# Prompt attention scores: two heads in the two row halves of the array, three products of 64 rows, no stacked copies

## The chip, the cores and the metric

The kernel runs on one core of one Trainium2 chip. The metric is device time in microseconds of one execution. The kernel before took 1777.86 us, the median of three runs (1774.98 to 1778.14).

## The reference

One inference step of a two-layer decoder trunk in float32: a prompt of 512 tokens and 8 sampled sequences of 8 new tokens each, which the kernel joins to T = 64 + 512 token columns. Each layer mixes tokens by three groups of heads (dilated attention with 8 heads of 64, two gated linear attentions), then applies a convolutional feed-forward part. The change touches the prompt's attention scores alone, the first product here:

```
s = jnp.einsum('nrbqhd,nrbkhd->nrbhqk', qb, kk) * (Dh ** -0.5)
...
s = jnp.where(valid[:, None], s + bias, -jnp.inf)
lse = jax.nn.logsumexp(s, axis=-1)
o = jnp.einsum('nrbhqk,nrbkhd->nrbqhd', jnp.exp(s - lse[..., None]), vv)
```

The three dilated branches are merged by their softmax denominators; the kernel gets the same from one softmax over all causal keys, with a bias that holds the slopes and the logarithm of how many branches read a key.

## The kernel before, in words

Features lie on the 128 partitions, tokens along the columns. A projection is a sum over 8 feature tiles. For near-float32 accuracy both operands are split into a high part in `F32R` and a low part, the difference, and three products are summed (`gemm`, lines 126 to 128): high x high, high x low, low x high. Weights come by DMA into `wraw`, ScalarE makes the high part (L107) and VectorE the low part (L108).

`mixing` first makes the gated linear heads (`hgrn_head`, `gla_tile`), then loops over four pairs of attention heads (`for p in range(4)`). A pair's 128 features are two heads of 64, the first on partitions 0 to 63, the second on 64 to 127. Per pair:

- the queries `qp` (128 x 512, evacuated at L796 and L798) and the keys `ka` (128 x 576, L574) are projected;
- the split copies for the score products are made. Before the change the two parts of a query are stacked on the partitions: for head `hb`, `q2[:, hb]` holds the high part on the head's own 64 partitions (ScalarE, L815) and the low part on the other 64 (GpSimd, L818). `kh[:, hb]` holds the high part of the keys on both halves (ScalarE, L816 and L817), `kl[:, hb]` the low part on both (GpSimd, L819 and L820). All three have one buffer, so the copies for a pair wait for the last score product of the pair before it;
- for each block `i` of 128 query rows and each head, two products on all 128 rows of the array (L832) give the scores of n = 128 (i + 1) keys: one with `kh` sums high x high and low x high, one with `kl` sums high x low and low x low;
- softmax of a block: VectorE adds the bias and takes the maximum (L839), negates it (L841), ScalarE takes the exponential with its sum (L842), VectorE the reciprocal (L843) and the multiplication by it (L844);
- TensorE transposes the block (L848), ScalarE and VectorE copy the transposes (L853, L851), and TensorE multiplies by the values (L857) into the head's half of the columns;
- then the sampled tokens' attention over the cached keys and values (L877, L881, L886 to L926), whose products use 32 columns of the array each.

The order on each engine is made ahead of time by a scheduler, which simulates the kernel: it takes the instructions as they become ready, so work of one pair, of the next pair's projections and of the cached keys is interleaved. Engines then run their lists in order. The score products and the levels of the gated linear heads share two PSUM banks of the kind `s`.

Of the kernel before, what the change touches and what calls it, by code (L numbers as in the profile page):

```python
# [8 lines left out]
F32 = mybir.dt.float32  # L9
F32R = mybir.dt.float32r  # L10
I32 = mybir.dt.int32
U8 = mybir.dt.uint8
AF = mybir.ActivationFunctionType
ALU = mybir.AluOpType
# [5 lines left out]
P = 128  # L20
# [3 lines left out]
TS = 64  # L24
TP = 512
# [48 lines left out]
def trunk_kernel(ctx: ExitStack, tc: tile.TileContext, I, O):  # L74
    nc = tc.nc
    V, S, G, PE, SP = nc.vector, nc.scalar, nc.gpsimd, nc.tensor, nc.sync
# [8 lines left out]
    def bank(tag, bufs):  # L85
        return ps.tile([P, 512], F32, name=f"ps_{tag}", tag=tag, bufs=bufs)
# [4 lines left out]
    def s_bank():  # L91
        return bank("s", 2)

    def t_bank():
        return bank("t", 2)

    def o_bank():
        return bank("o", 1)
# [46 lines left out]
    def mark(name, mm):  # L145

        placed[name] = mm.ins
# [415 lines left out]
    def mixing(l, act, first):  # L563
# [16 lines left out]
        with ExitStack() as mx:  # L580
            mp = mx.enter_context(tc.tile_pool(name=f"mp{l}", bufs=1, reuse_waits="tile"))
            ap = mx.enter_context(tc.tile_pool(name=f"ap{l}", bufs=1, reuse_waits="tile"))
# [197 lines left out]
            for p in range(4):  # L780
                qp = ap.tile([P, TP], F32, name="qp", tag="qp", bufs=QKB)
# [19 lines left out]
                ka = ap.tile([P, T], F32, name="ka", tag="ka", bufs=2)  # L801
# [4 lines left out]

                q2 = ap.tile([P, 2, TP], F32R, name="q2", tag="q2", bufs=1)  # L810
                kh = ap.tile([P, 2, TP], F32R, name="kh", tag="kh", bufs=1)
                kl = ap.tile([P, 2, TP], F32R, name="kl", tag="kl", bufs=1)
                for hb in range(2):
                    r, o_ = (slice(64 * e, 64 * e + 64) for e in (hb, 1 - hb))
                    S.activation(q2[r, hb, :], qp[r, :], AF.Copy)  # L815
                    S.activation(kh[r, hb, :], ka[r, TS:], AF.Copy)  # L816
                    S.activation(kh[o_, hb, :], ka[r, TS:], AF.Copy)  # L817
                    G.tensor_tensor(q2[o_, hb, :], qp[r, :], q2[r, hb, :].bitcast(F32), ALU.subtract)  # L818
                    G.tensor_tensor(kl[r, hb, :], ka[r, TS:], kh[r, hb, :].bitcast(F32), ALU.subtract)  # L819
                    G.tensor_tensor(kl[o_, hb, :], ka[r, TS:], kh[r, hb, :].bitcast(F32), ALU.subtract)  # L820
                o = o_bank()
                wb = []
                for hb in range(2):
# [1 line left out]
                    mark(f"d{p}.b{hb}", SP.dma_start(wb[hb], I["pbias"][2 * p + hb]))  # L825
                for i in range(4):
                    n = (i + 1) * P
                    sb, pi, pT = [], [], []
                    for hb in range(2):
                        sb.append(s_bank())  # L830
                        for j, kk in enumerate((kh, kl)):
                            mm = PE.matmul(sb[hb][:, :n], q2[:, hb, i * P:(i + 1) * P], kk[:, hb, :n],  # L832
                                           start=j == 0, stop=j == 1)
                    mark(f"p{p}.{i}", mm)
                    for hb in range(2):
                        pi.append(sp.tile([P, 512], F32, name="pi", tag="pi", bufs=4))
                        w = pi[hb][:, :n]
                        mx_ = sp.tile([P, 4], F32, name="mx", tag="mx", bufs=8)
                        V.tensor_tensor_reduce(w, sb[hb][:, :n], wb[hb][:, 512 - n:512], 1.0, -3.0e38,  # L839
                                               ALU.add, ALU.max, mx_[:, 0:1])  # L840
                        V.tensor_scalar(mx_[:, 1:2], mx_[:, 0:1], -1.0, None, ALU.mult)  # L841
                        S.activation(w, w, AF.Exp, bias=mx_[:, 1:2], accum_out=mx_[:, 2:3])  # L842
                        V.reciprocal(mx_[:, 3:4], mx_[:, 2:3])  # L843
                        V.tensor_scalar(w, w, mx_[:, 3:4], None, ALU.mult)  # L844
                    for hb in range(2):
                        tb = t_bank()
                        for c in range(i + 1):
                            PE.transpose(tb[:, c * P:(c + 1) * P], pi[hb][:, c * P:(c + 1) * P], ident)  # L848
                        pT.append(sp.tile([P, 512], F32, name="pT", tag="pT", bufs=3))
                        if hb:  # L850
                            V.tensor_copy(pT[hb][:, :n], tb[:, :n])  # L851
                        else:
                            S.activation(pT[hb][:, :n], tb[:, :n], AF.Copy)  # L853
                    for c in range(i + 1):
                        for hb in range(2):
                            h = 2 * p + hb
                            PE.matmul(o[64 * hb:64 * hb + 64, i * P:(i + 1) * P], va[:, c, h * 64:(h + 1) * 64],  # L857
                                      pT[hb][:, c * P:(c + 1) * P], start=c == 0, stop=c == i)
# [12 lines left out]
                for half in range(2):  # L871
                    sb = s_bank()
                    sb2.append(sb)
                    for s in range(2):
                        kc = cache(I["ck"][l, p, half, s], f"k{half}{s}")
                        for i in range(4):
                            PE.matmul(sb[32 * i:32 * i + 32, :384], qs[:, 2 * i + s, :], kc[:, i, :],  # L877
                                      start=(s == 0), stop=(s == 1))
                for s in range(2):
                    for i in range(4):  # L880
                        mm = PE.matmul(sb[32 * i:32 * i + 32, 384:448], qs[:, 2 * i + s, :], ka[:, 0:TS],  # L881
                                       start=(s == 0), stop=(s == 1))
# [17 lines left out]
                mm = PE.transpose(tb[:TS, 256:384], pr[:, 768:832], ident)  # L900
# [4 lines left out]
                for s in range(2):  # L905
# [7 lines left out]
                    for i in range(4):  # L913
                        mm = PE.matmul(ob[32 * i:32 * i + 32, s * P:(s + 1) * P],
                                  sT[:TS, 768 + 32 * i:768 + 32 * i + 32], vas[:TS, p * P:(p + 1) * P],
                                  start=False, stop=True)
# [21 lines left out]
        for c in range(KT):  # L938
            col_tile(load_w(I["w_o"][l, c], 5 * P, name=f"wo{c}"), mh, ml, range(5),
                     lambda b, hf, t0, n, c=c: S.activation(y[c][:, t0:t0 + n], b[:, :n], AF.Copy))  # L940

        xpool = right_pool(f"x_{l + 1}")
        src = I["x"] if l == 0 else xdr
# [136 lines left out]
    for l in range(L):  # L1080
        xpool.release()
        ypool.release()
        y, ypool, xpool, act, first = mixing(l, act, first)
        act, first = ffn(l, y, act, first)
# [192 lines left out]
```

## Time and profile before

| What | Value |
|---|---|
| median of the three runs | 1777.86 us |
| profiled execution, its own time | 1782.31 us |
| its span | 1780.5 us |
| TensorE, products | 1703.4 us busy, 96% |
| VectorE | 1136.0 us, 64% |
| ScalarE | 745.9 us, 42% |
| GpSimd | 414.9 us, 23% |
| mean granted clock of TensorE | 0.978 |

Busy times are unions of an engine's instructions. A product's bar runs until its result is out, so the bars of neighbours overlap; how much TensorE spends on one product is read from the distance of two starts. A product of float32 operands appears as two passes in the trace, one of `F32R` operands as one. The form of a product names the part of the array first: 64*32 means 64 rows and 32 columns.

### The profile page before, as it was taken

The numbers are of one execution on the slowest core, as the hardware profiler recorded it, in microseconds if no ns is written. First come the engines' busy times: TensorE is split into PE (matmuls) and PEld (weight loads), VectorE is DVE, ScalarE is ACT, GpSimd is POOL, SyncE is SP. The second block draws the span as 40 slices with busy tenths as digits, with TensorE's granted clock in tenths as the row PEclk, the third lists the DMA queues.
The fourth block names the chain that finished last, engine by engine and source line by source line (L and its number), as shares of the span: only waits on it lengthen the run. The fifth ranks groups of instructions, "written<-read, shape, count | busy, mean of one in ns | idle before, by whom it ended". The sixth has DMA issues, their size and how long they took to land.

```text
span 1780.5 us, 36320 instructions
## 1 busy us (share of the span) xinstructions
PE 1703.4 (96%) x14688; PEld 1598.8 (90%) x14688; DVE 1136.0 (64%) x2515; ACT 745.9 (42%) x1265; POOL 414.9 (23%) x748
## 2 busy tenths in 40 slices
PE   7999989999899999999989999999998999999996
PEld 7888976689799999999988898867898999999996
DVE  6776665655885376476677757466568744754666
ACT  5654424554443333233456534154545433332331
POOL 3544321301420010010254534122024100100103
PEclk9999999999999999999989999899999999999998
DMA  5212225866262562542322222368553526527321
GB/s 176 73 60 69 86 76 210 310 221 246 98 213 79 191 225 83 213 178 73 108 86 86 65 64 88 116 222 307 203 211 130 187 75 236 187 75 270 124 90 54
DMA packets 64520, 260.95 MB, mean 147 GB/s; under 512 B 9536, under 2 KB 15968, under 8 KB 62816
## 3 DMA queue, kind: packets, MB, share of 16 engines
q1 hardware_dynamic: 64352, 258.62, 41.5%
q8 instruction: 116, 1.90, 0.4%
q14 instruction: 52, 0.43, 0.1%
HBM read 245.39 MB, written 80.31 MB: 183 GB/s over the span
## 4 chain that ended last, share of the span: by engine, by line
PE 83%; DVE 10%; ACT 4%; issue 2%; DMA 1%; POOL 0%; SPq 0%; POOLq 0%; DVEq 0%; ACTq 0%
PE ps_m L126 23%; PE ps_m L128 23%; PE ps_m L127 23%; PE ps_s L472 2%; DVE xl L297 2%; PE ps_o L857 1%; PE ps_s L832 1%; PE ps_o L911 1%; DVE y L338 1%; DVE work L417 1%; PE ps_m L622 1%; PE ps_t L848 1%; DMA wraw<-in_w_s 1%; DVE wlo L108 1%; PE ps_s L877 1%
## 5 line engine op out<-in xcount | busy, mean ns | idle before, releaser
L126 PE MATMUL ps_m<-xh,whi 128*128 128x256 f32 (+1 forms) x2240 | 673.9, 301 | 3.1 <-DVE work L574 2.0
L127 PE MATMUL ps_m<-xl,whi 128*128 128x256 f32 (+1 forms) x2240 | 671.8, 300 | 0.0
L128 PE MATMUL ps_m<-xh,wlo 128*128 128x256 f32 (+1 forms) x2240 | 669.8, 300 | 1.2 <-DVE wlo L108 1.2
L126 PEld LDWEIGHTS ps_m<-xh,whi 128*128 128x128 f32 x2240 | 430.8, 192 | 11.4 <-issue 6.1
L127 PEld LDWEIGHTS ps_m<-xl,whi 128*128 128x128 f32 x2240 | 431.2, 192 | 3.0 <-issue 1.9
L128 PEld LDWEIGHTS ps_m<-xh,wlo 128*128 128x128 f32 x2240 | 430.2, 192 | 4.0 <-issue 1.5
L107 ACT ACTIVATE whi<-wraw 128x1024 fp32r<-128x1024 f32 (+3 forms) x224 | 221.4, 991 | 384.8 <-PE ps_m L127 323.5
L108 DVE TENSOR_TENSOR wlo<-wraw,whi 128x1024 fp32r<-128x1024 f32 (+3 forms) x224 | 257.6, 1152 | 183.6 <-ACT whi L107 183.1
L126 PE MATMUL ps_m<-hh,whi 128*128 128x320 f32 (+1 forms) x704 | 208.7, 296 | 1.3 <-DVE y L370 1.3
L128 PE MATMUL ps_m<-hh,wlo 128*128 128x320 f32 (+1 forms) x704 | 208.0, 296 | 0.0
L127 PE MATMUL ps_m<-hl,whi 128*128 128x320 f32 (+1 forms) x704 | 207.6, 295 | 0.0
L126 PEld LDWEIGHTS ps_m<-hh,whi 128*128 128x128 f32 x704 | 132.5, 188 | 1.6 <-DVE y L370 1.6
L127 PEld LDWEIGHTS ps_m<-hl,whi 128*128 128x128 f32 x704 | 133.2, 189 | 0.0
L128 PEld LDWEIGHTS ps_m<-hh,wlo 128*128 128x128 f32 x704 | 132.2, 188 | 0.0
L993 DVE TENSOR_TENSOR u<-ps_m,rbc 128x256 f32<-128x256 f32 x84 | 35.5, 424 | 111.3 <-PE ps_m L128 111.2
L408 POOL TENSOR_TENSOR lev<-work 128x288 f32<-128x288 f32 (+1 forms) x60 | 50.0, 834 | 155.9 <-DVE work L720 39.6
L1029 ACT ACTIVATE hh<-c 128x64 fp32r<-128x64 f32 x88 | 34.2, 436 | 122.3 <-DVE c L1019 122.3
L1001 POOL COPY cso<-u 128x2 f32<-128x2 f32 x88 | 34.5, 392 | 205.8 <-DVE u L993 204.9
L983 POOL COPY u<-cso 128x16 f32<-128x16 f32 x88 | 24.0, 275 | 221.2 <-DVE u L989 178.2
L1009 DVE SCALAR_TENSOR_TENSOR c<-u,par,c 128x592 f32<-128x592 f32 x88 | 73.4, 834 | 2.6
L126 PE MATMUL ps_m<-whi,xh 128*128 128x256 f32 (+1 forms) x256 | 74.2, 290 | 0.0
L127 PE MATMUL ps_m<-wlo,xh 128*128 128x256 f32 (+1 forms) x256 | 73.4, 287 | 0.0
(286 smaller groups left out, 2866.1 us busy)
## 6 DMA issues: line engine op xcount, KB each, us to landing
wraw<-in_w_up SPq DMA_DIRECT2D x88, 512.0 KB, 3.6
kv<-in_ck SPq DMA_DIRECT2D x32, 768.0 KB, 6.9
kv<-in_cv SPq DMA_DIRECT2D x32, 768.0 KB, 6.5
out_ck<-in_ck SPq DMA_DIRECT2D x32, 768.0 KB, 7.0
out_cv<-in_cv SPq DMA_DIRECT2D x32, 768.0 KB, 6.4
wraw<-in_w_s SPq DMA_DIRECT2D x42, 512.0 KB, 3.4
wraw<-in_w_dn SPq DMA_DIRECT2D x32, 448.0 KB, 3.3
wraw<-in_w_v SPq DMA_DIRECT2D x12, 512.0 KB, 3.4
```

Of the source, the lines that this page charges most:

```text
L107: S.activation(hi[:, :n], raw[:, :n], AF.Copy)
L108: V.tensor_tensor(lo[:, :n], raw[:, :n], hi[:, :n].bitcast(F32), ALU.subtract)
L126: PE.matmul(out, ah, bh, start=(i == 0), stop=False)
L127: PE.matmul(out, ah, bl, start=False, stop=False)
L128: PE.matmul(out, al, bh, start=False, stop=(i == n - 1))
L297: V.scalar_tensor_tensor(self.l[k][:, t0:t0 + n], xt[k][:, t0:t0 + n], gnorm(l, which, k), self.h[k][:, t0:t0 + n].bitcast(F32), ALU.mult, ...
L408: G.tensor_tensor(ev[:, :, 0, :], ref, bv[:, :, 0, :], ALU.subtract)
L472: mm = PE.matmul(bp[64 * hh:64 * hh + 64, cp * nh * 32:(cp + 1) * nh * 32], xk[:, c0:c0 + 64], moving(c0), start=True, stop=True)
L993: V.tensor_tensor(u[:, 338:594], b[:, :n], R[:, t0:t0 + n], ALU.mult)
L1001: G.tensor_copy(cso[:, ui, 16:18], u[:, NU - 2:NU])
L1009: V.scalar_tensor_tensor(c, u[:, 2:NU], wc(2), c, ALU.mult, ALU.add)
L1029: S.activation(dh, src, AF.Copy)
```

## The change

`q2`, `kh` and `kl` with a plane for each head are replaced by four tiles `qh`, `ql`, `kh`, `kl` of 128 x 512, with both heads on their own partitions. ScalarE makes each high part in one instruction on 128 partitions, GpSimd each low part. A score block is now the sum of three products (high x high, high x low, low x high) on the 64 rows of the array on which the head lies; the low x low product is gone. In the text the heads alternate inside each of the three products.

```
-                q2 = ap.tile([P, 2, TP], F32R, name="q2", tag="q2", bufs=1)
-                kh = ap.tile([P, 2, TP], F32R, name="kh", tag="kh", bufs=1)
-                kl = ap.tile([P, 2, TP], F32R, name="kl", tag="kl", bufs=1)
-                for hb in range(2):
-                    r, o_ = (slice(64 * e, 64 * e + 64) for e in (hb, 1 - hb))
-                    S.activation(q2[r, hb, :], qp[r, :], AF.Copy)
-                    S.activation(kh[r, hb, :], ka[r, TS:], AF.Copy)
-                    S.activation(kh[o_, hb, :], ka[r, TS:], AF.Copy)
-                    G.tensor_tensor(q2[o_, hb, :], qp[r, :], q2[r, hb, :].bitcast(F32), ALU.subtract)
-                    G.tensor_tensor(kl[r, hb, :], ka[r, TS:], kh[r, hb, :].bitcast(F32), ALU.subtract)
-                    G.tensor_tensor(kl[o_, hb, :], ka[r, TS:], kh[r, hb, :].bitcast(F32), ALU.subtract)
+                qh, ql, kh, kl = (ap.tile([P, TP], F32R, name=m, tag=m, bufs=1) for m in ("qh", "ql", "kh", "kl"))
+                for hi, lo, src in ((qh, ql, qp), (kh, kl, ka[:, TS:])):
+                    S.activation(hi, src, AF.Copy)
+                    G.tensor_tensor(lo, src, hi.bitcast(F32), ALU.subtract)
...
-                    sb, pi, pT = [], [], []
-                    for hb in range(2):
-                        sb.append(s_bank())
-                        for j, kk in enumerate((kh, kl)):
-                            mm = PE.matmul(sb[hb][:, :n], q2[:, hb, i * P:(i + 1) * P], kk[:, hb, :n],
-                                           start=j == 0, stop=j == 1)
+                    sb, pi, pT = [s_bank(), s_bank()], [], []
+                    for j, (qq, kk) in enumerate(((qh, kh), (qh, kl), (ql, kh))):
+                        for hb in range(2):
+                            r = slice(64 * hb, 64 * hb + 64)
+                            mm = PE.matmul(sb[hb][:, :n], qq[r, i * P:(i + 1) * P], kk[r, :n],
+                                           start=j == 0, stop=j == 2)
```

The scheduler makes a new order from this. Lines behind the copies move up by 8: L832 becomes L824, L842 L834, L844 L836, L848 L840, L857 L849, L877 L869.

On TensorE, the last blocks (n = 512) of the first layer's second pair, before (`ps_s` are scores, `ps_t` transposes, `ps_o` outputs):

```order
L848 MATMUL ps_t<-con,pi 128x128 x2
L832 MATMUL ps_s<-kh,q_3498 128x512
L832 MATMUL ps_s<-kl,q_3498 128x512
L857 MATMUL ps_o<-pT,va 64x128
L848 MATMUL ps_t<-con,pi 128x128 x2
L832 MATMUL ps_s<-kh,q_3498 128x512
L832 MATMUL ps_s<-kl,q_3498 128x512
L857 MATMUL ps_o<-pT,va 64x128
L877 MATMUL ps_s<-kv,qs 32x384 x8
```

The same place in the changed kernel:

```order
L840 MATMUL ps_t<-con,pi 128x128 x2
L824 MATMUL ps_s<-kh,qh 128x512
L824 MATMUL ps_s<-kl,qh 128x512
L824 MATMUL ps_s<-kh,ql 128x512
L849 MATMUL ps_o<-pT,va 64x128
L840 MATMUL ps_t<-con,pi 128x128 x2
L824 MATMUL ps_s<-kh,qh 128x512
L824 MATMUL ps_s<-kl,qh 128x512
L824 MATMUL ps_s<-kh,ql 128x512
L849 MATMUL ps_o<-pT,va 64x128
L869 MATMUL ps_s<-kv,qs 32x384 x8
```

The three products of one head stand together, and a value product and two transposes stand between them and those of the other head.

On ScalarE, the handover from the second pair to the third in the first layer, before (`kh` and `q` are the copies, `pi` a softmax block):

```order
L842 ACTIVATE pi,mx<-pi,mx 128x384
L816 ACTIVATE kh<-ka 64x512
L817 ACTIVATE kh<-ka 64x512
L816 ACTIVATE kh<-ka 64x512
L817 ACTIVATE kh<-ka 64x512
L815 ACTIVATE q_3915<-qp 64x512 x2
L842 ACTIVATE pi,mx<-pi,mx 128x512 x2
L853 ACTIVATE pT<-ps_t 128x384
```

The same place in the changed kernel:

```order
L834 ACTIVATE pi,mx<-pi,mx 128x384 x2
L811 ACTIVATE qh<-qp 128x512
L811 ACTIVATE kh<-ka 128x512
L834 ACTIVATE pi,mx<-pi,mx 128x512 x2
L845 ACTIVATE pT<-ps_t 128x384
```

Two copies in place of six stand ahead of the two exponentials of the last block.

## Rows read from the trace of the kernel before

**Rows 1.** The page: TensorE's busy time; the chain that ended last, by engine.

```profile
PE 1703.4 (96%) x14688; PEld 1598.8 (90%) x14688; DVE 1136.0 (64%) x2515; ACT 745.9 (42%) x1265; POOL 414.9 (23%) x748
...
PE 83%; DVE 10%; ACT 4%; issue 2%; DMA 1%; POOL 0%; SPq 0%; POOLq 0%; DVEq 0%; ACTq 0%
```

**Rows 2.** Stretches: length, PE, PEld, DVE, ACT, POOL busy, clock, DMA.

```profile
280.00:395.00 115.00, 110.02 (x1222) 81.68 (x1223) 72.64 (x248) 60.53 (x137) 27.78 (x24) 0.97 0.68 250
1164.00:1276.00 112.00, 107.05 (x1218) 80.97 (x1218) 72.69 (x247) 59.75 (x135) 27.49 (x24) 0.98 0.71 256
...
960.00:1060.00 100.00, 97.82 (x1125) 90.19 (x1124) 68.69 (x162) 52.56 (x71) 42.51 (x52) 0.99 0.20 63
...
283.00:287.00 4.00, 3.88 (x11) 1.91 (x11) 3.03 (x15) 2.19 (x8) 0.00 (x0) 0.50 0.47 197
```

**Rows 3.** Timeline of TensorE at 367.8 us: start, length, what.

```profile
367.79 0.39 PE L832 MATMUL ps_s<-kl,q 128*128 128x512 f32 x1
368.02 0.28 PE L126 MATMUL ps_m<-xh,whi 128*128 128x256 f32 x1
368.14 0.28 PE L127 MATMUL ps_m<-xl,whi 128*128 128x256 f32 x1
```

**Rows 4.** Timeline of TensorE at 310.3 us.

```profile
310.28 0.42 PE L914 MATMUL ps_o<-vas,sT 64*32 64x128 f32 x8
310.64 0.44 PE L832 MATMUL ps_s<-kh,q 128*128 128x384 f32 x1
310.92 0.34 PE L832 MATMUL ps_s<-kl,q 128*128 128x384 f32 x1
311.09 0.34 PE L832 MATMUL ps_s<-kh,q 128*128 128x384 f32 x1
```

**Rows 5.** Timeline of TensorE at 316.8 us.

```profile
316.78 0.40 PE L832 MATMUL ps_s<-kl,q 128*128 128x512 f32 x1
317.11 0.43 PE L857 MATMUL ps_o<-pT,va 128*64 128x128 f32 x2
317.47 0.44 PE L848 MATMUL ps_t<-con,pi 128*128 128x128 f32 x2
```

**Rows 6.** Timeline of all engines, handover from second to third pair, first layer.

```profile
318.24 0.63 ACT L816 ACTIVATE kh<-ka 64x512 fp32r<-64x512 f32 x1 [0.46 <-PE ps_s L832]
...
319.24 0.14 DVE L841 TENSOR_SCALAR mx<-mx 128x1 f32<-128x1 f32 x1
...
322.15 0.72 ACT L842 ACTIVATE pi<-pi,mx 128x512 f32<-128x512 f32 x1
...
322.98 1.27 POOL L820 TENSOR_TENSOR kl<-ka,kh 64x512 fp32r<-64x512 f32 x1
...
323.20 1.34 DVE L844 TENSOR_SCALAR pi<-pi,mx 128x512 f32<-128x512 f32 x1
...
324.32 2.69 POOL L818 TENSOR_TENSOR q<-qp,q 64x512 fp32r<-64x512 f32 x2
...
325.71 1.58 DVE L844 TENSOR_SCALAR pi<-pi,mx 128x512 f32<-128x512 f32 x1
...
327.44 0.63 PE L848 MATMUL ps_t<-con,pi 128*128 128x128 f32 x4 [1.33 <-DVE pi L844]
...
328.36 0.33 PE L832 MATMUL ps_s<-kh,q 128*128 128x128 f32 x1
```

**Rows 7.** Instructions of line L530: GpSimd on 128x512 (ns min/median/max).

```profile
L530 POOL TENSOR_TENSOR sn<-s,al x10: 1032/1413/2032, 52.5 to 1105.8; 128x512 f32<-128x512 f32 x10
```

**Rows 8.** Timeline of VectorE in the fourth pair, first layer.

```profile
371.19 0.49 DVE L844 TENSOR_SCALAR pi<-pi,mx 128x512 f32<-128x512 f32 x1
```

**Rows 9.** VectorE by line and form, 280:395, then 1164:1276: busy us, mean ns.

```profile
L844 DVE TENSOR_SCALAR pi<-pi,mx 128x512 f32<-128x512 f32 x8 | 8.7, 1084 | 0.2
...
L844 DVE TENSOR_SCALAR pi<-pi,mx 128x512 f32<-128x512 f32 x8 | 9.3, 1162 | 0.2
```

**Rows 10.** Waits of TensorE, 280:395: us in total, times, longest.

```profile
PE ps_s L832 <- DVE mx L839: 1.4, 1, 1.4
```

## The prediction

> **What bounds the kernel now.** I began with the page's busy shares and its chain. TensorE is busy for 1703.4 of 1780.5 us, and 83% of the chain that ended last is TensorE's [rows 1]: extra work on TensorE adds to the time unless it falls into a wait. The next view is the busy time by stretch. The change lies in two stretches, one per layer, where the four pairs' prompt scores, softmax and the cached keys run: 280 to 395 us and 1164 to 1276 us [rows 2]. TensorE is busy there for 110.02 of 115 and 107.05 of 112 us, so 5.0 + 5.0 = 10.0 us are idle. Busy counts each product until its result is out, so I looked at single starts in the timeline to see what one product costs. In a run of products of one shape they start at a fixed distance: 512 columns take 0.23 us (367.79 to 368.02) and 256 take 0.12 us (368.02 to 368.14) [rows 3]; 384 take 0.17 us (310.92 to 311.09) [rows 4].
>
> **Where the shape of the array's part changes, it costs more.** The first 384-column score product behind products on 64 rows and 32 columns takes 0.28 us, the next one 0.17 us: entering costs 0.10 to 0.11 us [rows 4]. The last 512-column product ahead of products on 64 columns takes 0.33 us (316.78 to 317.11) where 0.23 is usual: leaving costs 0.10 us; the two passes of 128 columns behind it occupy 0.36 us where two at the 256's 0.12 would be 0.24, with an entry and a leaving in them [rows 3, 5]. Of the 0.12 us beyond that, about 0.09 belongs to leaving, which leaves 0.03 to 0.05 us for entering with 128 columns. The eight products on 64 rows, between neighbours on 128 rows with the same 32 columns on one side, take 0.36 us for two rounds [rows 4], so a change of rows alone pays like any other.
>
> The Trainium skill, "TensorEngine Tiling (Array Packing)", section Tiling Modes, says that changing the tiling mode, unlike changing the tile, drains the engine. The trace agrees (0.33 against 0.23 us). It speaks against this change: today's score products have the shape of the projections and of the transposes, the new ones have a shape that nothing beside them has. Without the rule the sum below would lack its second term.
>
> **The change part by part.**
>
> Products. Per pair and row block, 4 products on 128 rows become 6 on 64 rows: 2 more at each of 128, 256, 384 and 512 columns. No row shows a single-pass product on 64 rows. Above, its cost is bounded by the same columns on 128 rows; below, by nothing at all, if all of it ran beside the other head's. I take the same per column, 128 columns at the 256's 0.12: 2 x (0.12 + 0.12 + 0.17 + 0.23) = 1.28 us a pair, 10.2 us for 8 pairs.
>
> Side by side. The eight products of rows 4 need only two rounds, so parts of the array do work at once, at least column parts; row halves are not shown. But the order decides. The text of the kernel alternates the heads, the scheduled order does not: it gives all three products of one head and then three of the other, with transposes and value products between. In all of TensorE's order a score product is followed directly by one of the other half at 11 places only (two heads or two row blocks that touch). At most 11 x 0.11 = 1.2 us are won back. Term: +10.2 - 1.2 = +9.0 us.
>
> Changes of shape. Counted through TensorE's whole order, neighbours with different shapes are 476 before and 536 now; those at the score products rise from 44 to 110. Of the 60 more, 46 enter a product of over 128 columns. That is 60 x 0.09 for leaving, 46 x 0.10 for entering, 14 x 0.05 for entering with 128 columns: 5.4 + 4.6 + 0.7 = 10.7 us. Bounds: 0, if each falls where TensorE waits anyway, and 60 x 0.21 = 12.6 us.
>
> Copies. Per pair ScalarE loses four of six copies. One on 64 partitions takes 0.63 us [rows 6]; on 128 I take the same time, so 2.5 us a pair go. GpSimd loses four of six subtractions of 1.27 us [rows 6]; one on 128 partitions is bounded by the 1.27 us on 64 and by 1.41 us, the float32 product on 128x512 [rows 7]. So 7.6 us a pair become about 2.7. What hides this today is TensorE's other work, except at the handover to the next pair. The timeline shows one at 318 to 327 us [rows 6]: the copies start at 318.24; the maximum of the pair's last block is ready at 319.24 + 0.14, yet its exponential starts at 322.15, behind six copies. Then VectorE's multiplication on 128x512 takes 1.34 and 1.58 us beside GpSimd's subtractions, against 0.49 us where GpSimd is still [rows 8]. TensorE waits 1.33 us for the second of them. Over both stretches these 16 multiplications take 8.7 + 9.3 us [rows 9] where 16 x 0.49 = 7.8 would do: 10.2 us of VectorE time. In the new order one exponential stands ahead of the two copies and the other behind them at the first handover, both behind them at the other two, so the delay shrinks from 3.8 to about 1.3 us. What it is worth is only TensorE's wait: at least 0, at most the 10.0 us idle in both stretches. 1.4 us of each stretch is the opening wait for the first softmax (the row reads alike in both) [rows 10], which the copies don't cause. I take the rest as won: 2 x (5.0 - 1.4) = -7.2 us. The opening waits stay, and take in added products: -2.8 us. Late next is then the products' own order.
>
> Moves. Elsewhere the scheduler moves gate products past state products at the start of the second layer. TensorE is busy 97.82 of 100 us there [rows 2], so I cost it at 0, between -3 and +3 (the 2.2 us idle either lost or doubled, rounded up). New waits: the second and third products wait for both subtractions, and the value products behind them wait along; today a pair's first score starts at 328.36, over 1 us behind the end of the last subtraction at 324.32 + 2.69 = 327.01 [rows 6], and four subtractions fewer stand ahead of it now, so I price it at 0; if that cover went, it were 1.3 us a pair, 10 us.
>
> Sum: +9.0 + 10.7 - 7.2 - 2.8 = +9.7 us. On the profiled execution, 1782.31 us (span 1780.5 and 1.8 around it), this gives 1792.0; that execution stands 4.4 us above the median of the runs, 1777.86, so there it is 1787.6: **1788 us**, 0.5% slower.
>
> **The rivals.** A measurement of this kernel tells about 0.2%, 3.6 us, from no change.
>
> 1. The waits take in the work: half of the 19.7 us on TensorE falls behind softmax waits that remain. +9.9 - 7.2 = about +3, 1781 us. For it: TensorE's products stand in chains with VectorE. Against: only 10 us are idle in both stretches. 15%.
>
> 2. The other side: the softmax chain bounds the stretches, and the copies' relief decides. It does if more than 12.5 of the 19.7 us fall into waits. Then the copies' 3.8 - 1.3 = 2.5 us at six handovers come back, of which 10 at most are TensorE's idle time, and some 3 us of products remain: -7, 1771 us. For it: the 10.2 us of slowed VectorE time; against: TensorE's 0.96 busy share. 9%.
>
> 3. The halves run side by side in spite of the order, the engine taking the other half's products ahead. Then the 24 products of a pair take three rounds of each width, 3 x 0.64 = 1.92 us, where today's 16 take 4 x 0.64 = 2.56: 8 x -0.64 = -5.1 in place of +9.0. -5.1 + 10.7 - 7.2 = -1.6, 1776 us. It needs starts that leave the program's order, and the trace shows starts in order everywhere I looked. 8%. The Trainium skill, "TensorE: Matmul & The Clock Gate", section Why this matters for your kernels, has small-K products in distinct row groups run at once, with 3.07x for four; the same page has products start and end in program order. By the first alone this rival would be the forecast, by the second it falls away.
>
> 4. The clock. From 283 to 287 us the granted clock is 0.50, the 1.2 GHz level, behind a wait in sparse work [rows 2]. If products on half the rows let it fall like that for 4 us at each of 6 handovers, 24 us at half speed lose 12: 1800 us. Against it: the clock is 0.97 and 0.98 over the stretches although many products there already use 32 columns. 8%.
>
> The forecast has the remaining 60%, with a range of its own of 1782 to 1795 (the shape changes at half, or the copies worth 0).
>
> **How the numbers follow.** Faster by over 0.2% (under 1774.3): rival 2 and a little of rival 3, 0.09. Within 0.2% (up to 1781.4): rival 1's larger half, the rest of rival 3 and the forecast's lower edge, 0.20. Slower: 0.71. The range from 1776 to 1799 leaves out rival 2 and rival 4's upper part.
>
> **What would show it.** Score products of 384 and 512 columns 0.17 and 0.23 us apart, three to a head, with starts 0.01 us apart only at the 11 places: the first term. The last of a group ahead of a transpose 0.10 us longer: the second. VectorE's 128x512 multiplications near 0.5 to 1 us instead of 1.1 and 1.2, and handover waits gone: the third. Both stretches together should be some 10 us longer, the rest alike. It is wrong if the stretches get shorter, if products of both halves start together throughout, or if the difference lies in the second layer's start.

## The result, and the profile after

The changed kernel takes 1791.13 us (median of four runs, 1790.08 to 1792.4) beside 1778.0 us for the kernel before on the same chip: ratio 1.0077, 95% interval 1.0059 to 1.0094. It is slower by some 13 us; forecast were 1788 us and +9.7.

The changed kernel's page, TensorE's busy time and the chain that ended last (of before: [rows 1]):

```profile
PE 1722.7 (96%) x14752; PEld 1604.4 (90%) x14752; DVE 1122.1 (63%) x2515; ACT 719.4 (40%) x1229; POOL 369.6 (21%) x716
...
PE 85%; DVE 9%; ACT 2%; issue 1%; DMA 1%; POOL 0%; SPq 0%; POOLq 0%; DVEq 0%; ACTq 0%
```

VectorE, ScalarE and GpSimd are all less busy, TensorE is 19.3 us more busy, and its share of the chain has grown from 83 to 85%.

To see where the time went I cut every span at the same instructions: an attention stretch runs from the first score product of a layer's second row block to the last product that gathers the outputs of its cached keys (L925 of before). Lengths in us, from the starts of products in each trace; the last column is the time within either stretch at which TensorE's granted clock was 0.50:

| Kernel | ahead of the first stretch | first stretch | between | second stretch | behind | span | at half clock, first + second stretch |
|---|---|---|---|---|---|---|---|
| before | 280.6 | 113.6 | 769.9 | 111.8 | 504.6 | 1780.5 | 6.8 + 3.4 |
| after | 275.2 | 120.8 | 766.5 | 120.8 | 505.1 | 1788.3 | 10.2 + 10.2 |

Both stretches are longer, by 7.2 and 9.0 us, but what lies ahead of each is shorter, by 5.4 and 3.4 us. The second was not forecast. "Behind" is alike. Two rows per kernel say the same by engine; columns: stretch, length, then busy time of PE, PEld, DVE, ACT and POOL with their counts, granted clock, DMA share and GB/s. Of before, at these cuts:

```profile
280.63:394.26 113.63, 109.28 (x1217) 80.94 (x1218) 72.05 (x245) 60.10 (x135) 27.58 (x24) 0.97 0.69 251
1164.12:1275.96 111.84, 107.00 (x1218) 80.93 (x1218) 72.60 (x245) 59.75 (x135) 27.45 (x24) 0.98 0.71 255
```

Of after, with the part of each stretch in which the clock was at its lower level, 1.2 GHz:

```profile
275.16:395.96 120.80, 120.19 (x1248) 86.06 (x1248) 69.32 (x245) 51.72 (x123) 12.07 (x12) 0.96 0.64 236
1162.44:1283.23 120.79, 120.31 (x1247) 86.20 (x1248) 69.43 (x245) 51.73 (x123) 12.05 (x12) 0.96 0.65 236
278.50:288.70 10.20, 10.20 (x39) 4.59 (x40) 6.97 (x24) 4.73 (x12) 2.68 (x2) 0.50 0.32 97
1165.90:1176.10 10.20, 10.20 (x41) 4.63 (x40) 7.29 (x25) 4.75 (x12) 2.68 (x2) 0.50 0.29 99
```

TensorE was idle for 4.4 and 4.8 us of the stretches before and is for 0.6 and 0.5 us after. Its waits inside the stretches are gone, it works for longer all the same, and it works at half clock for 10.2 us of each stretch.

Single products, in the changed kernel's timeline of TensorE (start, length, what; of before: [rows 3 to 5]):

```profile
280.33 0.62 PE L824 MATMUL ps_s<-kl,qh 64*128 64x512 f32 x1
280.76 0.62 PE L824 MATMUL ps_s<-kh,ql 64*128 64x512 f32 x1
...
310.22 0.44 PE L824 MATMUL ps_s<-kh,qh 64*128 64x384 f32 x1
310.50 0.34 PE L824 MATMUL ps_s<-kl,qh 64*128 64x384 f32 x1
310.68 0.33 PE L824 MATMUL ps_s<-kh,ql 64*128 64x384 f32 x1
310.94 0.39 PE L126 MATMUL ps_m<-xh,whi 128*128 128x256 f32 x1
...
315.30 0.49 PE L824 MATMUL ps_s<-kh,qh 64*128 64x512 f32 x1
315.64 0.39 PE L824 MATMUL ps_s<-kl,qh 64*128 64x512 f32 x1
315.87 0.39 PE L824 MATMUL ps_s<-kh,ql 64*128 64x512 f32 x1
316.19 0.43 PE L849 MATMUL ps_o<-pT,va 128*64 128x128 f32 x2
```

A 64-row product costs what a 128-row one does: 0.18 us for 384 columns (310.50 to 310.68; 0.17 before) and 0.23 for 512 (315.64 to 315.87). Entering costs 0.10 to 0.11 us (0.28 in place of 0.17, 0.34 in place of 0.23), leaving 0.09 (0.26 and 0.32). The Trainium skill, "TensorEngine Tiling (Array Packing)", section Tiling Modes, has a change of mode drain the engine; these starts agree.

The first two rows lie in the time at half clock: 512 columns take 0.43 us there (280.33 to 280.76), nearly twice the 0.23. So time at half clock is counted below as costing half of itself; that is an estimate, for a wait does not get longer with a slower clock.

### The profile page after: what moved, and what is told of

Same layout as the page of the kernel before. It is cut to its first block, busy times and chain, and to the rows that moved or that the text cites. A ratio compares the mean times of both kernels' runs of the same rounds, so it can differ in the third digit from the quotient of the medians.

```text
span 1788.3 us, 36388 instructions
## 1 busy us (share of the span) xinstructions
PE 1722.7 (96%) x14752; PEld 1604.4 (90%) x14752; DVE 1122.1 (63%) x2515; ACT 719.4 (40%) x1229; POOL 369.6 (21%) x716
## 4 chain that ended last, share of the span: by engine, by line
PE 85%; DVE 9%; ACT 2%; issue 1%; DMA 1%; POOL 0%; SPq 0%; POOLq 0%; DVEq 0%; ACTq 0%
PE ps_m L126 23%; PE ps_m L128 22%; PE ps_m L127 22%; PE ps_s L824 2%; PE ps_o L849 2%; PE ps_s L472 2%; DVE xl L297 2%; PE ps_s L869 2%; PE ps_t L840 1%; DVE y L338 1%; PE ps_o L903 1%; PE ps_m L622 1%; DMA wraw<-in_w_s 1%; DVE wlo L108 1%; DVE work L417 1%
## 5 line engine op out<-in xcount | busy, mean ns | idle before, releaser
L1021 ACT ACTIVATE hh<-c 128x64 fp32r<-128x64 f32 x88 | 34.2, 436 | 122.2 <-DVE c L1011 122.2
L128 PE MATMUL ps_m<-whi,xl 128*128 128x256 f32 (+1 forms) x256 | 73.5, 287 | 0.0
```

The lines of the kernel that those rows point to most:

```text
L128: PE.matmul(out, al, bh, start=False, stop=(i == n - 1))
```

## The experiments

My theory: over both stretches the 64 extra products and the 60 extra changes of shape cost about ten us each, and the lighter copies win some of it back at the handovers between pairs. Rivals: the copies are worth nothing, or much more; one of the two costs is absorbed. Each kernel below has four to eleven runs beside the kernel before on the same chip. The table continues the one above (span of the profiled execution):

| Kernel | ahead | first | between | second | behind | span | half clock |
|---|---|---|---|---|---|---|---|
| two products, 128 rows | 275.1 | 112.7 | 764.6 | 109.4 | 504.6 | 1766.4 | 6.8 + 3.4 |
| three products, 128 rows | 275.9 | 113.5 | 767.2 | 114.2 | 505.8 | 1776.6 | 3.4 + 3.4 |
| two products, 64 rows | 273.5 | 116.4 | 760.8 | 118.0 | 504.9 | 1773.6 | 10.2 + 10.2 |
| heavy copies, every pair | 281.3 | 120.7 | 773.6 | 119.4 | 505.6 | 1800.6 | 10.2 + 10.2 |
| heavy copies, first pair | 282.1 | 121.6 | 770.4 | 120.7 | 504.8 | 1799.7 | 13.7 + 10.2 |
| after once more | 275.3 | 120.8 | 765.3 | 122.2 | 504.9 | 1788.6 | 10.2 + 13.7 |
| halves in turns | 274.0 | 113.1 | 766.2 | 111.7 | 504.2 | 1769.1 | 6.8 + 3.4 |
| blocks kept whole | 278.3 | 131.9 | 767.1 | 130.9 | 507.2 | 1815.5 | 37.1 + 29.0 |
| before, VectorE subtracts | 279.1 | 109.8 | 767.3 | 110.3 | 504.9 | 1771.4 | 0.0 + 0.0 |
| turns, VectorE subtracts | 273.2 | 111.7 | 765.5 | 113.8 | 504.7 | 1768.9 | 3.4 + 10.2 |

Single executions lie some us off their medians (before's +4, that of two products on 128 rows +4), so sizes are given by both.

**1. The light copies alone.** After's copies; two products per head over all 128 rows, so the scores sum both heads.

```
-                    for j, (qq, kk) in enumerate(((qh, kh), (qh, kl), (ql, kh))):
-                        for hb in range(2):
...
+                    for hb in range(2):
+                        for j, (qq, kk) in enumerate(((qh, kh), (qh, kl))):
+                            mm = PE.matmul(sb[hb][:, :n], qq[:, i * P:(i + 1) * P], kk[:, :n],
+                                           start=j == 0, stop=j == 1)
```

> The copies of the changed kernel (two on ScalarE, two on GpSimd per pair, 128 partitions) with the products of before: two per head on all 128 rows (each sums both heads' scores, so the scores are not the reference's). TensorE's work is as before, only the copies are light. Theory (products + shape changes cost 19.7 us, lighter copies win back 7): about 1771 us, 7 us under before. Rival (the copies are hidden, the changed kernel's 13 us are all that products and shapes cost): 1778 us, like before.

Measured: 1764.54 us, ratio 0.9925 [0.9912, 0.9937]. The copies win 13.3 us, more than either said. But the table has only 0.9 and 2.4 us of it in the stretches; 5.5 lie ahead of the first and 5.3 between the two (net of a loss there, see Moves further down).

```profile
275.06:387.79 112.73, 112.08 (x1222) 82.80 (x1223) 68.32 (x246) 53.90 (x126) 11.80 (x12) 0.97 0.69 257
1152.43:1261.85 109.42, 108.58 (x1222) 82.14 (x1223) 69.26 (x246) 54.03 (x126) 11.66 (x12) 0.98 0.71 264
```

PE's idle time is gone here too (0.7 and 0.8 us), but its bars have grown by 2.8 and 1.6 us, so the stretches hardly shrink. In part these are the 5 and 4 products more that the order puts between the cuts; the rest is open.

**2. The third product.** As 1, with three products on 128 rows; the edit is against the changed kernel.

```
-                            r = slice(64 * hb, 64 * hb + 64)
-                            mm = PE.matmul(sb[hb][:, :n], qq[r, i * P:(i + 1) * P], kk[r, :n],
+                            mm = PE.matmul(sb[hb][:, :n], qq[:, i * P:(i + 1) * P], kk[:, :n],
                                            start=j == 0, stop=j == 2)
```

> The changed kernel with its three products per head on all 128 rows in place of 64 (scores of both heads summed, not the reference's). It adds the 64 products but no change of shape: about 485 changes in TensorE's order against 536. Theory: 10 us over the light copies with two products, so about 1781 us, and 10 us under the changed kernel. Rival (changes of shape fall into waits, products alone cost): like the changed kernel, 1791 us. Rival (products are hidden, shapes alone cost): 1771 us.

Measured: 1774.46 us, 0.9974 [0.9961, 0.9987]. Against 1, the ratios differ by 0.0049, 8.7 us (9.9 by the medians); the stretches grow by 5.6 us, and by 7.3 once the 3.4 us less at half clock, worth half of that, are set aside.

**3. The changes of shape.** As after without its third product: two on 64 rows, with 531 changes of shape through TensorE's order where 1 has 483 (before 476, after 536).

```
-                    for j, (qq, kk) in enumerate(((qh, kh), (qh, kl), (ql, kh))):
+                    for j, (qq, kk) in enumerate(((qh, kh), (qh, kl))):
...
-                                           start=j == 0, stop=j == 2)
+                                           start=j == 0, stop=j == 1)
```

> The changed kernel without its third product (the queries' low part times the keys' high part is left out): two products per head on 64 rows, 531 changes of shape. Theory: 10 us under the changed kernel, 1781 us, and 10 us over two products on 128 rows. Rival (shapes alone cost): 1791 us. Rival (products alone cost): 1771 us.

Measured: 1775.53 us, 0.9982 [0.9973, 0.9991], 10.1 us over 1 by the ratios. The stretches grow by 12.3 us; what lies between them is 3.8 us shorter, because the scheduled order there is before's and not after's (see Moves). In the first stretch:

```profile
275.70:285.90 10.20, 10.20 (x41) 4.24 (x40) 7.57 (x28) 5.47 (x15) 2.50 (x2) 0.50 0.47 153
```

The clock is at 0.50 for 10.2 us, as in after, with a third fewer score products. Of the 12.3 us, (10.2 + 10.2 - 6.8 - 3.4) / 2 = 5.1 are the clock's by the estimate above and 7.2 the 48 changes', 0.15 us for each.

**4. The heavy copies under the new products.** After's products; before's six copies and six subtractions on 64 partitions for each pair, those that nothing needs going to scratch tiles.

```
-                for hi, lo, src in ((qh, ql, qp), (kh, kl, ka[:, TS:])):
...
+                for hb in range(2):
+                    r, o_ = (slice(64 * e, 64 * e + 64) for e in (hb, 1 - hb))
+                    S.activation(qh[r, :], qp[r, :], AF.Copy)
+                    S.activation(kh[r, :], ka[r, TS:], AF.Copy)
+                    S.activation(kx[o_, :], ka[r, TS:], AF.Copy)
+                    G.tensor_tensor(ql[r, :], qp[r, :], qh[r, :].bitcast(F32), ALU.subtract)
+                    G.tensor_tensor(kl[r, :], ka[r, TS:], kh[r, :].bitcast(F32), ALU.subtract)
+                    G.tensor_tensor(ky[o_, :], ka[r, TS:], kh[r, :].bitcast(F32), ALU.subtract)
```

> The changed kernel's products with the number and size of copies of before: six on ScalarE and six subtractions on GpSimd per pair, 64 partitions each (four of them write scratch tiles nobody reads). Theory (the light copies win 13 us, whatever the products are): 1804 us. Rival (the copies only mattered with the products of before): 1791 us.

Measured: 1802.81 us, 1.0142 [1.0122, 1.0161], 11 us over after. The stretches are as long as after's (120.7 and 119.4 beside 120.8 and 120.8), although each pair has eight more copies and subtractions; the time lies ahead (+6.1) and between (+7.1). TensorE's order is not quite after's, with 549 changes of shape instead of 536.

**5. The heavy copies for each layer's first pair only.** The first pair's copies are made ahead of the stretch, beside the gated linear heads.

```
+                if p == 0:
...
+                    for hb in range(2):
...
+                else:
+                    for hi, lo, src in ((qh, ql, qp), (kh, kl, ka[:, TS:])):
```

The left-out lines are those of 4.

> The changed kernel with the copies of before for the first pair of each layer alone; the other three pairs keep the light copies. TensorE's shape changes and score groups are as in the changed kernel (536 and 55). Theory (most of what the copies win lies ahead of the attention stretches, where the first pair's subtractions on GpSimd slow VectorE's multiplications of the gated heads, L417): some 9 to 10 us over the changed kernel, 1800 us. Rival (it lies at the handovers between pairs, as the prediction had it): 1 to 3 us over, 1793 us.

Measured: 1803.54 us, 1.0146 [1.0133, 1.016]: the same as 4. Here TensorE's order has after's 536 changes of shape. Under the products on 64 rows all that the copies win, they win at the first pair of each layer; at the handovers they win nothing that can be measured. TensorE's wait for VectorE's L417, which leads to the cause further down, is back at before's 6.0 us.

**6. After once more.** No edit; a second sample beside 4, 5 and others.

> The changed kernel once more, on the chip of the three runs below, to have them side by side: 1.0077 of before again (1791 us). In its profile the granted clock at the start of both attention stretches shows whether the long stay at half speed (10.2 us in each, where kernels with products on 128 rows had 3.4 or 6.8) comes with the products on 64 rows: yes by that theory, 3.4 or 6.8 us if it is chance.

Measured: 1791.61 us, 1.0079 [1.0066, 1.0092]. The clock is at half for 10.2 and 13.7 us, not for 3.4 or 6.8.

**7. Before, with the first pair's subtractions on VectorE.** If GpSimd's subtractions slow VectorE at the first pair, moving them away ends it.

```
-                    G.tensor_tensor(q2[o_, hb, :], qp[r, :], q2[r, hb, :].bitcast(F32), ALU.subtract)
+                    (V if p == 0 else G).tensor_tensor(q2[o_, hb, :], qp[r, :], q2[r, hb, :].bitcast(F32), ALU.subtract)
...
```

> The kernel before with one edit: the first pair's six subtractions of each layer on VectorE instead of GpSimd (0.5 to 0.7 us each on 64x512, some 4 us of VectorE time a layer). Theory (GpSimd's subtractions slow VectorE's multiplications L417, 5.1 us a layer, and TensorE waits and falls to its lower clock): most of the first pair's 12 us comes back, about 1769 us. Rival (the length of VectorE's own queue decides, wherever the subtractions stand): 1778 us.

Measured: 1774.82 us, 0.9981 [0.9972, 0.999], 3.4 us won, less than half of what the theory said. Its rows stand below, with the first pair's.

**8. Halves in turns.** After's work, with each of a block's six products bound behind the one before it, alternating heads. In TensorE's order products of the other half now follow each other at 144 places instead of 11.

```
+                    prev = None
...
+                            with behind(prev):
+                                mm = PE.matmul(sb[hb][:, :n], qq[r, i * P:(i + 1) * P], kk[r, :n],
+                                               start=j == 0, stop=j == 2)
+                            prev = mm.ins
...
```

> The changed kernel with the six products of a block bound to take turns on TensorE: first head, second head, first head, and so on. In the order 16 of 32 blocks then stand whole, the others as one and five; the half changes at 144 places instead of 11, and the shape at 516 instead of 536. Theory (row halves work side by side when the order lets them): some 11 us less for products and 4 us less for shapes than the changed kernel, about 1776 us. Rival (row halves run one after the other): only the shapes, 1787 us. Rival (the turns hold back the first head's softmax, whose wait then decides): 1791 us or more.

Measured: 1770.92 us, 0.996 [0.9947, 0.9972]: 20 us under after, and faster than before. A block of 384 columns, both heads, in its timeline of TensorE:

```profile
303.10 0.44 PE L826 MATMUL ps_s<-kh,qh 64*128 64x384 f32 x2
303.38 0.34 PE L826 MATMUL ps_s<-kl,qh 64*128 64x384 f32 x2
303.56 0.33 PE L826 MATMUL ps_s<-kh,ql 64*128 64x384 f32 x2
303.82 0.39 PE L127 MATMUL ps_m<-xl,whi 128*128 128x256 f32 x1
```

Each score row is a pair (x2) that starts 3 ns apart. Six products take 0.72 us, what three take in after (310.22 to 310.94): the second head is free. In all, 75 score products start within 10 ns of the one ahead of them. The stretches are back to 113.1 and 111.7 us, the time at half clock to before's:

```profile
274.02:387.08 113.06, 111.77 (x1253) 82.93 (x1254) 65.92 (x245) 53.85 (x126) 12.12 (x12) 0.97 0.68 253
...
276.00:282.80 6.80, 6.68 (x27) 3.98 (x29) 5.00 (x23) 3.55 (x11) 0.12 (x1) 0.50 0.34 139
```

So the stretches are 16.8 us shorter than after's. By estimate 5.1 of these go with the clock and some 4 with the 20 changes of shape fewer; the rest, some 8, is the products side by side.

**9. Blocks kept whole.** As 8, and a block's first product also waits for the last transpose of the block before it, so that 22 of 32 blocks stand undivided instead of 16 and there are 472 changes of shape instead of 516.

```
+                held = None
...
-                    prev = None
+                    prev = held
...
+                            held = PE.transpose(tb[:, c * P:(c + 1) * P], pi[hb][:, c * P:(c + 1) * P], ident).ins
```

> Turns as in the run before, and from the second block of a pair on a block's first product is put behind the transposes of the block before it, by which time both score banks are free: 22 of 32 blocks stand whole instead of 16, changes of shape fall from 516 to 472. Theory (TensorE's issue decides in the stretch): 44 x 0.18 = 8 us less than with turns alone, less what the later start of the scores costs: about 1765 us. Rival (the softmax chain now decides, and scores held behind transposes lengthen it): 1771 us or more.

Measured: 1815.66 us, 1.0217 [1.0202, 1.0233]. The stretch is 131.9 us long with 17.0 us idle; its longest waits there (in all, times, longest):

```profile
PE ps_t L844 <- DVE pi L840: 7.1, 4, 3.3
```

The transposes of a block wait for its softmax with no scores of the next block ahead of them. Another 5.5 us of waits of the same transposes are put down to the reciprocal ahead of that multiplication (L839). In 8 the wait shown comes to 0.8 us; the softmax chain decides once scores cannot run ahead. The clock is at half for 37.1 us of this stretch, in four pieces.

**10. 8 and 7 together.**

```
-                    G.tensor_tensor(lo, src, hi.bitcast(F32), ALU.subtract)
+                    (V if p == 0 else G).tensor_tensor(lo, src, hi.bitcast(F32), ALU.subtract)
```

> Turns (the version that beat both, 1771 us) with the first pair's two subtractions of each layer on VectorE as well. Theory: the 2.2 us a layer that TensorE still waits for L417 go, 1 to 4 us under the turns alone: about 1768 us. Rival (VectorE is as late with two more instructions of 0.7 us): 1771 us.

Measured: 1771.73 us, 0.9963 [0.9951, 0.9976]: no different from 8. TensorE's wait for L417 stays, 2.1 us where 8 has 2.2: this move wins nothing where two subtractions are left of six.

## Why the prediction was right, and where it was not

Direction and size came out, the size in part by luck: one step failed, two terms had been left at nothing, and these errors offset each other.

**Products: right.** +9.0 was the term; +8.7 by the ratios of 2 and 1, 7.3 us in their stretches at equal clock. The starts above bear out the price per column, which no row of before had shown.

**Side by side: the places right, the argument not.** Eight score products start within 11 ns of the one ahead, of 11 places forecast. But the prediction had them start in program order. At 299.23 us the order holds three products of 128 columns of one head, then three of 256 columns of the other; the timeline of after:

```profile
299.23 0.39 PE L824 MATMUL ps_s<-kh,qh 64*128 64x128 f32 x2
299.39 0.35 PE L824 MATMUL ps_s<-kl,qh 64*128 64x128 f32 x2
299.50 0.35 PE L824 MATMUL ps_s<-kh,ql 64*128 64x128 f32 x2
```

Each row merges one product of either head; by single records those of 128 columns start at 299.227, .392 and .502 and those of 256 at .237, .459 and .577. The two halves advance each on its own. That the order is three and then three, as the prediction says, fits its 11 changes of half: the trace has eight groups of six like this one and three places more where one head's three follow the other's (two at 275, one at 1162 us); six that take turns would have five changes each. The Trainium skill, "TensorE: Matmul & The Clock Gate", section The mechanism, has products start and end in program order; these starts disagree. All three products of the narrower block are free at such a place, some 2.6 us at eight (8 x 3 x 0.11, from .392 to .502) where 1.2 was forecast. Rival 3 still failed, because transposes and value products stand between the heads, not because the engine keeps to the order. Experiment 8 is that rival, made by hand: it was priced at 1776 us and measured 1771.

**Changes of shape: right.** +10.7 for 60 changes, 0.18 each; 7.2 us for 48 in experiment 3, the clock apart. Experiment 3 also has eight places where halves run side by side, two products each; with the 8 x 2 x 0.11 = 1.8 us that these win (an estimate), a change costs 0.19 us.

**The clock, rival 4: in part true.** Neither the products nor the shapes explain all of the 19.5 us by which after's stretches exceed those of experiment 1; 7.3 + 7.2 leave 5.0, and the clock accounts for 5.1. In the ten stretches with mostly serial 64-row products (after twice, 3, 4, 5) the clock was at half for 10.2 us or more; in the kernels on 128 rows, for 0 to 6.8, and with the halves in turns (8 and 10) for 3.4 to 10.2; in 9, with its waits, for 29.0 and 37.1. In the ten it didn't fall at six handovers as the rival had it, but once, within 4 us of the stretch's start. That it went with these products is what the runs show; why is open.

**Copies: the step that failed.** "What it is worth is only TensorE's wait", between 0 and 10 us, taken as 7.2 at the handovers; the opening waits were to absorb 2.8 more. Measured are 13.3 us in all (1). By the spans 3.3 of it lie in the stretches, and under after's products nothing that can be measured (4 and 5); the rest is won at each layer's first pair, which the prediction never priced: "what hides this today is TensorE's other work, except at the handover". The cover that it named was missing there. Between the second and the third pair the handover did get lighter, as the timeline of all engines in after shows (of before: [rows 6]):

```profile
317.76 0.63 ACT L811 ACTIVATE qh<-qp 128x512 fp32r<-128x512 f32 x1 [0.71 <-PE ps_s L824]
...
318.47 1.29 POOL L812 TENSOR_TENSOR ql<-qp,qh 128x512 fp32r<-128x512 f32 x1 [23.52 <-ACT qh L811]
318.62 1.34 DVE L836 TENSOR_SCALAR pi<-pi,mx 128x384 f32<-128x384 f32 x1
...
322.12 0.47 DVE L836 TENSOR_SCALAR pi<-pi,mx 128x512 f32<-128x512 f32 x1
```

The multiplication on 512 columns takes 0.47 us where it took 1.34. But the subtractions now lie beside the 384-column ones (1.34 us at 318.62). By line and form (busy us, mean ns), after from 275 to 396 us:

```profile
L836 DVE TENSOR_SCALAR pi<-pi,mx 128x384 f32<-128x384 f32 x8 | 7.0, 880 | 0.0
L836 DVE TENSOR_SCALAR pi<-pi,mx 128x512 f32<-128x512 f32 x8 | 5.2, 645 | 0.2
```

and of before, from 280 to 395, the form that [rows 9] left out:

```profile
L844 DVE TENSOR_SCALAR pi<-pi,mx 128x384 f32<-128x384 f32 x8 | 4.0, 499 | 0.0
```

Together 12.2 us after and 4.0 + 8.7 = 12.7 before. The forecast sign (512 columns at 0.5 to 1 us) appeared and meant little: the contention had moved. Nor did the opening wait, which stands right ahead of the stretch, take products in; its 1.4 us are there as before ([rows 10]), the longest of these two waits of after:

```profile
PE ps_s L824 <- DVE mx L831: 1.7, 2, 1.4
```

Now the first pair. VectorE's multiplications for the gated linear heads' levels (L417), and beside them GpSimd's subtractions, in before (VectorE's timeline, then GpSimd's):

```profile
226.37 3.75 DVE L417 TENSOR_TENSOR work<-lev,work 32x256 f32<-32x256 f32 x4
...
239.92 4.67 DVE L417 TENSOR_TENSOR work<-lev,work 32x256 f32<-32x256 f32 x4
...
226.63 2.75 POOL L818 TENSOR_TENSOR q<-qp,q 64x512 fp32r<-64x512 f32 x2
239.75 1.29 POOL L820 TENSOR_TENSOR kl<-ka,kh 64x512 fp32r<-64x512 f32 x1
241.12 1.33 POOL L819 TENSOR_TENSOR kl<-ka,kh 64x512 fp32r<-64x512 f32 x1
242.51 1.34 POOL L820 TENSOR_TENSOR kl<-ka,kh 64x512 fp32r<-64x512 f32 x1
```

in after, then in experiment 7:

```profile
227.21 2.79 DVE L417 TENSOR_TENSOR work<-lev,work 32x256 f32<-32x256 f32 x4
...
238.35 1.74 DVE L417 TENSOR_TENSOR work<-lev,work 32x256 f32<-32x256 f32 x4
```

```profile
229.14 1.80 DVE L417 TENSOR_TENSOR work<-lev,work 32x256 f32<-32x256 f32 x4
...
240.42 0.69 DVE L820 TENSOR_TENSOR kl<-ka,kh 64x512 fp32r<-64x512 f32 x1
241.74 1.75 DVE L417 TENSOR_TENSOR work<-lev,work 32x256 f32<-32x256 f32 x4
```

Four of them take 1.75 us alone and 4.67 beside subtractions. TensorE waits for them; its waits from 221 to 250 us, of before and of after:

```profile
PE ps_s L472 <- DVE work L417: 6.0, 2, 3.7
```

```profile
PE ps_s L472 <- DVE work L417: 2.2, 2, 1.4
```

and behind each of these waits of before the granted clock was down, which after's clock of 1.00 over 221 to 250 us shows no more. Of before, then of after:

```profile
231.80:235.20 3.40, 3.40 (x19) 3.06 (x19) 2.85 (x6) 0.63 (x1) 0.89 (x2) 0.50 0.21 77
245.40:248.80 3.40, 3.40 (x21) 3.07 (x18) 2.85 (x5) 0.00 (x0) 0.00 (x0) 0.50 0.02 5
```

```profile
221.00:250.00 29.00, 26.63 (x292) 23.69 (x291) 22.85 (x47) 6.50 (x10) 8.44 (x8) 1.00 0.18 58
```

So the loss in the first layer is 3.8 us of waiting and about 6.8 / 2 = 3.4 of clock, 7.2 us where the table has 5.4. Experiment 7 shows GpSimd's subtractions to be what slows VectorE, but it won only 3.4 us: the six subtractions, 0.70 us each, then stand in VectorE's own queue, four of them right ahead of the level at 241.74, and TensorE still waits 3.6 us for L417. Its order has the moves besides, which cost 2.2 us in its trace. How much of the remaining gain comes from ScalarE's four copies fewer was not tried.

**Moves: priced too low.** They were costed at 0, between -3 and +3. Experiment 3 has before's order between the stretches; the other ten profiles have the moved one. The column "between" hides what that does, for the first pair of the second layer lies in it too. Cut once more, at the same product of the second layer (L472, ahead of its first pair), of before, then of after:

```profile
394.26:1090.45 696.19, 678.17 (x5467) 658.45 (x5466) 446.90 (x885) 296.89 (x470) 161.67 (x332) 0.99 0.38 133
1090.45:1164.12 73.67, 66.27 (x662) 59.76 (x661) 47.48 (x121) 16.00 (x26) 18.67 (x17) 0.91 0.31 109
395.95:1097.30 701.35, 680.11 (x5467) 660.16 (x5467) 448.30 (x885) 291.69 (x466) 158.61 (x332) 0.99 0.39 132
1097.30:1162.44 65.14, 61.34 (x665) 55.07 (x664) 43.50 (x121) 13.45 (x22) 13.45 (x13) 1.00 0.35 123
```

Up to the cut the same 5467 products take 5.2 us more in after, 3.2 of them idle; behind it, at the first pair, after is 8.5 us shorter. With before's order the first part takes 696.2 and 696.0 us (before and 3), with the moved one 698.4 to 702.3. The clock alone doesn't explain it: before and experiment 4 both spend 17.1 us of it at half, and 4 takes 700.7. So the moves cost some 2 to 6 us; no run tests them by themselves.

The account in spans, before to after: copies -17.9 and moves +3.8 (together the -14.1 of experiment 1), products +7.3, shapes +7.2, clock +5.1, and 2.4 outside the stretches that no experiment explains: +7.9, where the two spans differ by 7.8. Forecast for the same were -10.0, 0, +9.0, +10.7, 0 and 0. The copies' gain was taken 8 us too small, the products and shapes 5 too large together, and the clock and the moves, left out of the sum, made up for it: that is luck.

The account by the ratios closes less well. Experiments 1 to 3 give -13.3 + 8.7 + 10.1 = +5.5, and some 4 more because 3 lacks the moves; measured are +13.7. Some 4 us stay open, about what the intervals of the ratios allow together.

## What to carry to other kernels

Price work that is taken off an engine at every place where it runs, not where its wait is easiest to see: ask at each which engine it slows beside it and who waits for that one. Products on half of the array's rows paid here only where the other half's stood next to them in the order that the engine gets; write that order down, for a scheduler that takes what is ready did not keep it. Keep the scores of the next block ahead of the transposes of this one while doing so. And where a scheduler makes a new order from every edit, compare kernels between the same two products, and look at whether the order between these is the same.

## What the runs showed of the hardware

- Products in the two row halves run side by side, 3 ns apart, at no loss of speed, and each half advances by itself past the program order (299.227 to 299.577 us above). Experiment 8, with 75 such pairs, is 20 us faster than the changed kernel, of which some 8 in the stretches are theirs by estimate; fewer changes of shape and less time at half clock are the rest there.
- A product on 64 rows costs per column what one on 128 does: 0.23 us for 512 columns. At half clock it costs 0.43.
- With 384 and 512 columns, entering or leaving products on 64 rows costs 0.09 to 0.11 us beside the usual distance of starts (384 columns: 0.28 and 0.26 in place of 0.17).
- VectorE's four `tensor_tensor` on 32x256 go from 1.75 to 4.67 us beside GpSimd's subtractions, a `tensor_scalar` on 128x512 from 0.49 to 1.58 [rows 6, 8].
